# A 4096 x 4096 matmul with GELU: one partial product of the first group moved forward, set aside and put back into PSUM

## The chip, the cores and the metric

One core of a Trainium2 chip. The metric is the device time of one execution in microseconds (us), the median of several. Engine names: PE is the matmul engine (PEld its weight loads), DVE the vector engine, ACT the scalar engine, POOL the engine that issues most loads, SP the one that issues stores.

## The reference

```
x = np.matmul(a, b)               # a, b: 4096 x 4096, float32
return 0.5 * x * (1 + np.tanh(np.sqrt(2 / np.pi) * (x + 0.044715 * x**3)))
```

The result is 4096 x 4096 in float32.

## The kernel before

A and B are each cut into four quarters, A11 to A22 and B11 to B22, and most of the output is made with Strassen's seven products (M1 to M7) instead of eight. Operands are float16, sums in PSUM are float32. The output is made in groups: a group takes 512 rows of each half of A (four tiles of 128 rows, `i` from 0 to 3) and 512 columns of each half of B, and makes four blocks, c11, c12, c21 and c22. There are 4 by 4 groups; inside a group the 2048-long sum is cut into two chunks of 1024 (`c` = 0 and 1). So "A12_0" is A12's first chunk for the group, "A12_1" its second. The whole program is written in Python as a list of `steps`; for each step the lists `before` and `tasks` hold the loads, transposes and sums that are issued ahead of that step's matmuls. Each engine runs its instructions in the order in which they are written.

**The first group** differs from the others. While its data still come in, its first chunk is multiplied without Strassen: eight plain products (`PLAIN`), each of two steps, steps 0 to 15, in `plain` (matmuls on L524, 16 in a step). Its second chunk then goes through Strassen's products, steps 16 to 29: M3, M5, M7, M1, M4, M2, M6, two steps each (`multiply`, matmuls on L493). Group 1 begins at step 30.

The plain products, in the kernel's order (`PLAIN`, L101): c12 by A11 B12; c11 by A11 B11; c21 by A21 B11; c12 by A12 B22; c11 by A12 B21; c21 by A22 B21; c22 by A21 B12; c22 by A22 B22. All products but those of c11 go through the same four PSUM banks ("Y", one for each row tile `i`); c11 has the other four ("X"). Between two products in Y the banks must be read out:

- c12's first part: copied by ACT into tiles x1 (`keep`, L604); its second part: added to them by DVE (`tt`, L646).
- c11: both parts are summed in the X banks, and DVE then adds them to x1's tiles.
- c21's first part: copied by ACT (L540); its second part: added by DVE.
- c22: both parts, being neighbours, are summed in PSUM, and DVE subtracts the sum from x1's tiles.

The products with `True` in their last place go by rows: their first step makes the row tiles 0 and 1 in full, the second the tiles 2 and 3. The others make half of the sum for all four tiles in each step.

**Loading.** A line of the table at L761, such as `(9, "T22_0 W22_0 A12_1+B21_1a B21_1b")`, names what is issued ahead of a step: `A..`/`B..` a load, `T..` a transpose, `W..` weighing, `S..` a sum of two blocks of B. All loads are issued by POOL in the order written (L280); a load that must wait for its buffer holds back those behind it.

- `load_a` brings a chunk of A (1 MB as float16) into a stage tile. There are two stage tiles (`bufs=2`), used in turn. The one exception is `THIRD = ("22", 1)`: A22_1 goes into the four tiles "x7", which hold M7's parts later; in the profile these are named x.
- `turn_a` (T) transposes it on DVE into the block that PE reads (L244).
- `weigh_first` (W) squares each of the 16 rows of blocks in the stage tile on ACT, in place, with a sum along the row (L294; an ACTIVATE and a read of the accumulator for each of 16). It is part of a check of the inputs' sizes, on which the kernel's path depends. Only when all 16 are done is the stage tile free for the next load.

So the chunk that takes a stage tile next waits for the squares of the chunk before: A22_0 for W21_0, A11_1 for W12_0, A12_1 for W22_0, A21_1 for W11_1.

`make_sums` (L455) makes Strassen's sums of blocks on DVE; by default the loop at the end of `half_path` calls it two steps ahead (`AHEAD = 2`). The first of them, for M3, is B12_1 + B22_1; M5 needs A11_1 - A12_1, M7 needs A12_1 - A22_1 and B21_1 + B22_1, and M1 (A11_1 - A22_1 and B11_1 - B22_1) is the first to need B11_1.

Of the kernel before, what the change touches and what calls it, by code (L numbers as in the profile page):

```python
# [22 lines left out]
RT = 4  # L23
# [76 lines left out]

PLAIN = [  # L101
    ("12", "11", "12", False), ("11", "11", "11", False), ("21", "21", "11", True),
    ("12", "12", "22", False), ("11", "12", "21", False), ("21", "22", "21", True),
    ("22", "21", "12", True), ("22", "22", "22", True),
]
N_PLAIN = 2 * len(PLAIN)

# [1 line left out]
C21_FIRST = (0, 5, QPH - 1)  # L109
# [50 lines left out]
def half_path(  # L160
# [9 lines left out]
    nc = tc.nc  # L170
# [243 lines left out]
    kept = {}  # L414
# [57 lines left out]
    N_RAW = NNB + 2  # L472
# [3 lines left out]
    post = {}  # L476
# [21 lines left out]
    def warm():  # L498
        z = pool.tile([P, NC], F16, name="zeros", tag="bS", bufs=AHEAD + 1)
        nc.vector.memset(z[:, :], 0.0)  # L500
        for i in range(RT):
            bank(0, "X", i)
            bank(0, "Y", i)
        for _ in range(N_WARM):
            nc.tensor.matmul(
                banks["X", RT - 1][:, :], z[:, :P], z[:, :], start=True, stop=True, skip_group_check=True
            )

    def plain(n):

        (quad, oa, ob, by_rows), h = PLAIN[n // 2], n % 2
        chain = "X" if quad == "11" else "Y"
        seen = [x for x in range(len(PLAIN)) if PLAIN[x][0] == quad]
        sa, sb = a_tiles[0, oa, 0], b_tiles[0, ob, 0]
        sa = sa.rearrange("p jj (m e) -> p jj m e", e=2)
        tiles = [(j, e) for j in range(NJ // 2) for e in range(2) if by_rows or e == h]
        for i in range(h * RT // 2, (h + 1) * RT // 2) if by_rows else range(RT):
            acc = banks[chain, i]
            kept = quad in ("11", "22")
            start = (n // 2 == seen[0] or not kept) and (by_rows or h == 0)  # L520
            stop = (n // 2 == seen[-1] or not kept) and (by_rows or h == 1)
            c = f"c{quad}"
            for j, e in tiles:
                nc.tensor.matmul(  # L524
                    acc[:, :], sa[:, j, i * P : (i + 1) * P, e], sb[:, 2 * j + e, :],
                    start=start and (j, e) == tiles[0], stop=stop and (j, e) == tiles[-1],
                    skip_group_check=True,
                )
            if not stop:
                continue  # L530
            if not kept and n // 2 == seen[1]:
                tt(post[c, i], post[c, i], acc, ALU.add)
            elif quad == "12":
                post[c, i] = keep("x1", acc, RT)
            elif quad == "11":
                tt(post["c12", i], post["c12", i], acc, ALU.add)
            elif quad == "21":
                tag = ("energy1", "energy2", "square", "square")[i]
                t = pool.tile([P, W], BF16, name="c21", tag=tag, bufs=1 + (i > 1)).bitcast(F32)
                nc.scalar.copy(out=t[:, :], in_=acc[:, :])  # L540
                post[c, i] = t
            else:
                tt(post["c12", i], post["c12", i], acc, ALU.subtract)

# [57 lines left out]
    def keep(tag, src, bufs):  # L602
        t = pool.tile([P, NC], F32, name=tag, tag=tag, bufs=bufs)
        nc.scalar.copy(out=t[:, :], in_=src[:, :])  # L604
        return t
# [39 lines left out]
    def tt(o, x, y, op):  # L645
        nc.vector.tensor_tensor(out=o[:, :], in0=x[:, :], in1=y[:, :], op=op)  # L646
# [84 lines left out]
    for gi in range(1, len(groups)):  # L731
        s = 0
# [9 lines left out]
    before = {}  # L742

    def step_number(gi, s, q):
        gi, s = gi + s // NP, s % NP
        if (gi, s, q) in position:
            return position[gi, s, q]
        s0 = max(x for x in SPLITS if x <= s)
        return position[gi, s0, PAIR[0][1]] + (s - s0) * len(SPLIT) + 2 * q
# [10 lines left out]

    for n, whats in (  # L761
        (0, "A11_0 B12_0 T11_0 W11_0 B11_0 A21_0 A12_0 B22_0 B21_0"),
        (4, "T21_0 W21_0 A22_0"),
        (6, "T12_0 W12_0"),
        (8, "A11_1+B12_1+B22_1"),
        (9, "T22_0 W22_0 A12_1+B21_1a B21_1b"),
        (14, "T11_1 W11_1 A22_1 B11_1"),
        (16, "T12_1"),
        (17, "A21_1"),
        (18, "S2 S3 T22_1 W22_1:0-4"),  # L770
        (19, "W22_1:4-8"),
        (20, "W22_1:8-12"),
        (21, "W22_1:12-16"),
        (23, "T21_1"),
        (34, "W12_1:0-1"),
        (35, "W12_1:1-2"),
        (36, "W12_1:2-3"),
        (37, "W12_1:3-4"),
        (38, "W12_1:4-5"),
        (39, "W12_1:5-6"),  # L780
        (40, "W12_1:6-7"),
        (41, "W12_1:7-8"),
        (42, "W12_1:8-9"),
        (43, "W12_1:9-10"),
        (44, "W12_1:10-11"),
        (45, "W12_1:11-12"),
        (46, "W12_1:12-13"),
        (47, "W12_1:13-14"),
        (48, "W12_1:14-15"),
        (49, "W12_1:15-16"),  # L790
        (50, "W21_1:0-1"),
        (51, "W21_1:1-2"),
        (52, "W21_1:2-3"),
        (53, "W21_1:3-4"),
        (54, "W21_1:4-5"),
        (55, "W21_1:5-6"),
        (56, "W21_1:6-7"),
        (57, "W21_1:7-8"),
        (58, "W21_1:8-9"),
        (59, "W21_1:9-10"),  # L800
        (60, "W21_1:10-11"),
        (61, "W21_1:11-12"),
        (62, "W21_1:12-13"),
        (63, "W21_1:13-14"),
        (64, "W21_1:14-15"),
        (65, "W21_1:15-16"),
    ):
        for what in whats.split():
            half = what[-1] == "0" and what != "A11_0" or what in ("A22_1", "T22_1")
            if what[0] == "S":  # L810
                before.setdefault(n, []).append((make_sums, (0, 2, int(what[1]), "bS")))
                continue
            if what[0] == "W":
                xs = range(*(int(x) for x in what[6:].split("-"))) if what[6:] else range(NX)
                before.setdefault(n, []).append((weigh_first, (what[1:3], int(what[4]), xs)))
                continue
            for h in (0, 1) if half else (None,):
                args = [
                    (x[0], (0, x[1:3], int(x[4]), "ab".index(x[5]) if x[5:] else h))
                    for x in what.split("+")  # L820
                ]
                if what[0] == "T":
                    before.setdefault(n, []).append((turn_a, args[0][1]))
                    if what == "T22_1":
                        for q in range(QPH // 2, QPH):
                            before[n].append((make_sums, (0, 2, q, "aS", h)))
                else:
                    pairs = [({"A": load_a, "B": load_b}[x], xs) for x, xs in args]
                    before.setdefault(n, []).append((load, pairs))
# [57 lines left out]
    for nb, gi in last_raw.items():  # L887
# [6 lines left out]
        for x, piece in enumerate(pieces):  # L894
            n = position[gi, 0, 0] + max(x // 2, x - n_two)
            if two:
                n = position[gi - 1, 0, 0] + TWO_GROUPS[x]
# [251 lines left out]
    for gi in range(N_RAW, len(groups)):  # L1149
# [5 lines left out]
        for made, first_s, first_q, made_nb, name in MAKES:  # L1155
            s0, x = PLACE[name]
            ps = [p for p in SPLIT if not isinstance(SPLIT[p][2], str)]
            n = step_number(made, first_s, first_q)
# [4 lines left out]
        for n in mine:  # L1163
            _, s, q = steps[n]
# [33 lines left out]
    with tc.manual_schedule():  # L1198
        warm()
        table = pool.tile([P, 1], F32, name="table", tag="table")  # L1200
        nc.vector.memset(table[:, :], 0.0)
        nc.scalar.activation(table[:, :], table[:, :], ACT.Gelu_apprx_tanh)
        for n, step in enumerate(steps):
            for fn, args in before.get(n, ()):
                fn(*args)
            if n + AHEAD < len(steps):
                gi, s, q = steps[n + AHEAD]
                if s >= 0 and gi < N_RAW and step != C21_FIRST:
                    make_sums(gi, s, q)
            for fn, args in tasks.get(n, ()):  # L1210
                fn(*args)
            if step[:2] != (0, 2):
                flush()
            combine()
            if step[1] < 0:
                plain(n)
            elif step[2] in SPLIT:
                multiply_split(*step)
            else:
                multiply(*step)  # L1220
            if step == C21_FIRST:
                make_sums(*steps[n + AHEAD])
            if step == (0, 2, QPH - 1):
                flush()
        flush()
# [3 lines left out]
def kernel(tc: tile.TileContext, a: bass.AP, b: bass.AP, out: bass.AP):  # L1229
    stands = half_path(tc, a, b, out)  # L1230
    with tc.If(stands == 0):
        general_path(tc, a, b, out)
# [30 lines left out]
```

## Time and profile before

| | |
|---|---|
| median of 8 runs | 1558.95 us (1554.63 to 1563.45) |
| the profiled execution, its own time | 1560.27 us |
| its span, first to last instruction | 1558.6 us |
| granted PE clock, mean | 0.999 |

| stretch (us) | PE busy | DVE busy | ACT busy | POOL busy | GB/s |
|---|---|---|---|---|---|
| 38 to 60 | 22.00 | 10.25 | 9.94 | 16.85 | 192 |
| 70 to 76 | 6.00 | 4.75 | 2.23 | 4.54 | 195 |
| 76 to 83 | 7.00 | 6.67 | 3.49 | 6.70 | 126 |
| 83 to 90 | 6.60 | 5.16 | 5.50 | 5.93 | 155 |

Rows of the profile in order of time read: start in us, duration in us, engine, line, operation, output<-input, shape, count, and in square brackets the idle time of that engine just before, with what ended it. Rows of waits read: the engine, what it was to write, its line, what it waited for, then us in total, times, and the longest. A line such as L646 is a helper's and is used from many places; the names of the tiles tell which. PE's ends are modelled, so two neighbouring rows may overlap by some tenths of a microsecond.

### The profile page before, as it was taken

Reading aid. Unit: us, or ns where it says so; the run is one execution under the profiler, and the core shown is the slowest. Engines: PE = TensorE matmul, PEld = TensorE weight load, DVE = VectorE, ACT = ScalarE, POOL = GpSimd, SP = SyncE. Lnnn points to the kernel's source line nnn. Section 1 sums busy time; section 2 is a strip of 40 time slices with the busy share of each in tenths; the row PEclk is TensorE's granted clock in tenths of the full one; section 3 lists DMA queues with packets and bytes.
Section 4 is the critical chain, followed back from the end, with each engine's and each line's share of the span. In section 5 each row is a group of like instructions: output and inputs, shape, how many; then the busy total and the mean of one; then the engine's idle time right before and its main releaser. Section 6 shows DMA issues by size and latency. Waiting matters only on the chain. (4 is left out here: it accounts for less than half of the span.)

```text
span 1558.6 us, 22302 instructions
## 1 busy us (share of the span) xinstructions
PE 1543.9 (99%) x8110; PEld 793.7 (51%) x8110; DVE 1139.8 (73%) x1359; ACT 600.7 (39%) x1323; POOL 464.0 (30%) x830
## 2 busy tenths in 40 slices
PE   9999999999999999999999999999998999999998
PEld 4444444444444444444444444645646457677674
DVE  1598888999878888755657667867739677867674
ACT  5347555366633641211543211122344423232232
POOL 7764333431123211222322211211333212132130
PEclk9999999999999999999999999999999999999999
DMA  9999999994799988999799988868999958688693
GB/s 177 191 206 263 299 316 289 291 211 82 207 252 290 303 290 306 360 375 326 199 341 279 415 305 340 313 267 272 303 202 342 325 181 286 235 281 314 232 331 115
DMA packets 201909, 425.21 MB, mean 273 GB/s; under 512 B 20416, under 2 KB 102592, under 8 KB 199744
## 3 DMA queue, kind: packets, MB, share of 16 engines
q0 software_dynamic: 140448, 261.15, 65.7%
q1 hardware_dynamic: 61200, 162.43, 27.4%
q8 instruction: 66, 1.08, 0.3%
q14 instruction: 51, 0.42, 0.1%
q10 hardware_dynamic: 144, 0.13, 0.0%
HBM read 336.60 MB, written 162.53 MB: 320 GB/s over the span
## 5 line engine op out<-in xcount | busy, mean ns | idle before, releaser
L493 PEld LDWEIGHTS <-aS 128*128 128x128 f16 x4192 | 409.6, 98 | 497.3 <-issue 3.4
L493 PE MATMUL accX<-bK,aS 128*128 128x512 f16 x1536 | 334.0, 379 | 0.0
L976 DVE TENSOR_TENSOR aS<-aT 128x2048 f16<-128x2048 f16 x182 | 217.6, 1221 | 94.6 <-PE accX L493 63.0
L493 PEld LDWEIGHTS <-aT 128*128 128x128 f16 x1600 | 156.6, 98 | 188.1
L962 POOL DMA_DIRECT2D bK<-k_M x228 | 121.0, 535 | 419.4 <-PE accX L493 116.9
L280 POOL DMA_DIRECT2D bR<-in_b_dram x320 | 173.7, 546 | 215.0 <-DMA bR<-in_b_dram 96.5
L294 ACT ACTIVATE stage<-stage 128x512 f16<-128x512 f16 (+1 forms) x304 | 163.3, 542 | 112.6 <-DVE aT L244 78.7
L493 PE MATMUL accY<-bK,aS 128*128 128x512 f16 x896 | 195.2, 379 | 0.4 <-DVE x L646 0.3
L637 ACT ACTIVATE x<-x 128x512 f32<-128x512 f32 x124 | 75.7, 629 | 236.6 <-DVE x L646 236.6
L455 DVE TENSOR_TENSOR aS<-aT 128x2048 f16<-128x2048 f16 (+1 forms) x112 | 134.2, 1202 | 29.8 <-PE accX L493 18.6
L575 PEld LDWEIGHTS <-aS 128*128 128x128 f16 x1440 | 141.4, 98 | 27.4 <-issue 4.5
L493 PE MATMUL accX<-bS,aS 128*128 128x512 f16 x704 | 153.3, 379 | 0.4 <-ACT m L604 0.4
L455 DVE TENSOR_TENSOR bS<-bR 128x2048 f16<-128x2048 f16 x110 | 133.7, 1220 | 21.4 <-PE accX L493 13.6
L604 ACT COPY x<-accX 128x512 f32<-128x512 f32 x116 | 67.5, 586 | 194.5 <-PE accX L493 193.8
L336 ACT ACTIVATE square<-bR 128x1024 bf16<-128x1024 f16 x120 | 123.1, 1050 | 42.1 <-DVE energy L646 40.9
L244 DVE STREAM_TRANSPOSE aT<-stage 128x1024 uint32<-128x1024 uint32 (+1 forms) x59 | 73.5, 1279 | 70.8 <-DMA stage<-in_a_dram 70.8
L280 POOL DMA_DIRECT2D stage<-in_a_dram x136 | 80.2, 595 | 138.4 <-ACT stage L294 100.7
L976 DVE TENSOR_TENSOR bS<-bK 128x2048 f16<-128x2048 f16 x70 | 84.4, 1219 | 25.6 <-DMA k_split<-bS 25.5
L493 PE MATMUL accY<-bK,aT 128*128 128x512 f16 x448 | 97.8, 379 | 0.0
L493 PE MATMUL accX<-bK,aT 128*128 128x512 f16 x448 | 97.8, 379 | 0.0
L604 ACT COPY m<-accX 128x512 f32<-128x512 f32 x76 | 43.5, 582 | 126.2 <-PE accX L493 100.3
L646 DVE TENSOR_TENSOR x<-accY,x 128x512 f32<-128x512 f32 x116 | 77.5, 689 | 17.9 <-ACT y L637 11.1
(76 smaller groups left out, 1539.1 us busy)
## 6 DMA issues: line engine op xcount, KB each, us to landing
bK<-k_M POOLq DMA_DIRECT2D x264, 512.0 KB, 9.7
bK<-k_split POOLq DMA_DIRECT2D x90, 512.0 KB, 6.5
bR<-in_b_dram POOLq DMA_DIRECT2D x320, 128.0 KB, 7.6
k_M<-bS SPq DMA_DIRECT2D x80, 512.0 KB, 6.7
k_split<-bS SPq DMA_DIRECT2D x70, 512.0 KB, 7.0
out_dram<-y SPq DMA_DIRECT2D x131, 256.0 KB, 6.1
out_dram<-x SPq DMA_DIRECT2D x124, 256.0 KB, 7.1
stage<-in_a_dram POOLq DMA_DIRECT2D x112, 256.0 KB, 9.0
```

Of the source, the lines that this page charges most:

```text
L244: nc.vector.transpose(dst[:, :, x, :], src)
L280: nc.gpsimd.dma_start(out=dst, in_=src)
L294: nc.scalar.activation(src, src, ACT.Square, accum_out=dst)
L336: nc.scalar.activation(t[:, :], src, ACT.Square)
L455: nc.vector.tensor_tensor(out=x, in0=y, in1=z, op=ALU.add if o[2] > 0 else ALU.subtract)
L493: nc.tensor.matmul(acc[:, :], sa[:, j // 2, i * P : (i + 1) * P, j % 2], sb[:, j, :], start=start and j == 0, stop=stop and j == 3, skip_g ...
L575: nc.tensor.matmul(banks[chain, i][:, :] if wide else out, sa[:, j // 2, r * P : (r + 1) * P, j % 2], sb[:, : NC] if wide else sb[:, j * N ...
L604: nc.scalar.copy(out=t[:, :], in_=src[:, :])
L637: nc.scalar.activation(y[:, :], src[:, :], ACT.Gelu_apprx_tanh)
L646: nc.vector.tensor_tensor(out=o[:, :], in0=x[:, :], in1=y[:, :], op=op)
L962: nc.gpsimd.dma_start(out=dst, in_=kept_unit(*key[1:])[:, x * w : (x + 1) * w])
L976: nc.vector.tensor_tensor(out=t, in0=y, in1=z, op=ALU.add if op > 0 else ALU.subtract)
```

## The change

Four things, all in the first group:

1. A21 by B12 (c22's first part) moves from the seventh to the fourth place among the plain products. c12's second, c11's second and c21's second part each move one place back. A22 by B22 stays last.
2. c22's two parts are no longer neighbours in the Y banks. The first is copied by ACT into tiles of the tag x7 after steps 6 and 7; just ahead of A22 by B22 (steps 14 and 15) ACT copies it back into the Y banks, and the matmuls add to it.
3. The table of what is issued ahead of which step is rewritten: the squares of A21_0 are spread over steps 4 to 7, T12_0 and W12_0 stand at step 8 instead of 6, T22_0 at 12 instead of 9, the squares of A22_0 are spread over steps 13 to 16, A12_1's load stands ahead of B21_1's instead of being interleaved with its first half, A22_1's and B11_1's loads are at 12 instead of 14, and T11_1 at 15 instead of 14.
4. M3's sums are no longer made two steps ahead by the loop but by new entries: S02 at step 15, S03 at 16 (the sums of B alone), X02 and X03 at 16 (the rest of `make_sums`, which finds the sum made).

A22_1's stage in the x7 tiles is in the kernel before already; `THIRD` isn't touched.

```
 PLAIN = [
     ("12", "11", "12", False), ("11", "11", "11", False), ("21", "21", "11", True),
-    ("12", "12", "22", False), ("11", "12", "21", False), ("21", "22", "21", True),
-    ("22", "21", "12", True), ("22", "22", "22", True),
+    ("22", "21", "12", True), ("12", "12", "22", False), ("11", "12", "21", False),
+    ("21", "22", "21", True), ("22", "22", "22", True),
 ]
...
-            stop = (n // 2 == seen[-1] or not kept) and (by_rows or h == 1)
+            stop = (n // 2 == seen[-1] or quad != "11") and (by_rows or h == 1)
             c = f"c{quad}"
+            if quad == "22" and not start:
+                nc.scalar.copy(out=acc[:, :], in_=post.pop((c, i))[:, :])
...
                 post[c, i] = t
+            elif start:
+                post[c, i] = keep("x7", acc, RT)
             else:
                 tt(post["c12", i], post["c12", i], acc, ALU.subtract)
...
         (0, "A11_0 B12_0 T11_0 W11_0 B11_0 A21_0 A12_0 B22_0 B21_0"),
-        (4, "T21_0 W21_0 A22_0"),
-        (6, "T12_0 W12_0"),
-        (8, "A11_1+B12_1+B22_1"),
-        (9, "T22_0 W22_0 A12_1+B21_1a B21_1b"),
-        (14, "T11_1 W11_1 A22_1 B11_1"),
-        (16, "T12_1"),
+        (4, "T21_0 W21_0:0-2 A22_0"),
+        (5, "W21_0:2-6"),
+        (6, "W21_0:6-11"),
+        (7, "W21_0:11-16"),
+        (8, "T12_0 W12_0 A11_1+B12_1+B22_1"),
+        (9, "A12_1 B21_1"),
+        (12, "T22_0 A22_1 B11_1"),
+        (13, "W22_0:0-6"),
+        (14, "W22_0:6-8"),
+        (15, "T11_1 S02 W22_0:8-10"),
+        (16, "S03 X02 X03 W22_0:10-16 W11_1 T12_1"),
         (17, "A21_1"),
-        (18, "S2 S3 T22_1 W22_1:0-4"),
+        (18, "S22 S23 T22_1 W22_1:0-4"),
...
             if what[0] == "S":
-                before.setdefault(n, []).append((make_sums, (0, 2, int(what[1]), "bS")))
+                before.setdefault(n, []).append((make_sums, (0, int(what[1]), int(what[2]), "bS")))
+                continue
+            if what[0] == "X":
+                before.setdefault(n, []).append((make_sums, (0, int(what[1]), int(what[2]))))
                 continue
...
-                if s >= 0 and gi < N_RAW and step != C21_FIRST:
+                if s >= 0 and gi < N_RAW and step != C21_FIRST and (gi, s) != (0, 0):
                     make_sums(gi, s, q)
```

## The prediction

> **What bounds the kernel now.** I read the page first, then PE's waits up to 220 us, then PE, DVE, POOL and ACT in order of time up to 125 us. PE is the bound:
>
> ```profile
> span 1558.6 us, 22302 instructions
> PE 1543.9 (99%) x8110; PEld 793.7 (51%) x8110; DVE 1139.8 (73%) x1359; ACT 600.7 (39%) x1323; POOL 464.0 (30%) x830
> ```
>
> The matmuls stay as they are, so only PE's idle time (1558.6 - 1543.9 = 14.7 us) can move. PE's waits up to 220 us, apart from the one for the first instruction (us, times, longest):
>
> ```profile
> PE accY L524 <- DMA bR<-in_b_dram: 1.3, 2, 0.8
> PE accY L493 <- DVE x L646: 1.1, 1, 1.1
> PE accY L493 <- DVE bS L455: 0.5, 1, 0.5
> PE accX L493 <- ACT m L604: 0.4, 1, 0.4
> ```
>
> They add up to 3.3 us, the most that can be gained. From 120 to 220 us PE has no gap, so a shift of PE at 120 us stays to the end. PE in order of time:
>
> ```profile
> 27.34 7.07 PE L524 MATMUL accY<-bR,aT 128*128 128x512 f16 x32
> 35.24 7.07 PE L524 MATMUL accY<-bR,aT 128*128 128x512 f16 x32 [0.83 <-DMA bR<-in_b_dram]
> 49.05 20.88 PE L524 MATMUL accY<-bR,aT 128*128 128x512 f16 x96
> 69.77 7.07 PE L493 MATMUL accY<-bS,aT 128*128 128x512 f16 x32
> ```
>
> A product of 32 matmuls takes 6.9 us, a step 3.45. The 0.83 us is a wait for B22_0. DVE:
>
> ```profile
> 49.76 2.44 DVE L646 TENSOR_TENSOR x<-x,accX 128x512 f32<-128x512 f32 x4
> 63.32 2.31 DVE L244 STREAM_TRANSPOSE aT<-stage 128x2048 uint32<-128x2048 uint32 x1 [6.41 <-DMA stage<-in_a_dram]
> 71.88 2.31 DVE L244 STREAM_TRANSPOSE aT<-stage 128x2048 uint32<-128x2048 uint32 x1 [1.22 <-DMA stage<-in_a_dram]
> 89.99 1.22 DVE L455 TENSOR_TENSOR bS<-bR 128x2048 f16<-128x2048 f16 x1 [1.70 <-DMA bR<-in_b_dram]
> ```
>
> DVE waits for the loads A11_1, A12_1 and B11_1. From 90 to 120 us it is busy 29.9 of 30 us, and PE's gaps at 112 and 117 us are waits for it: loads set DVE, DVE sets PE. POOL issues the loads:
>
> ```profile
> 1.56 2.73 POOL L280 DMA_DIRECT2D stage<-in_a_dram  x4 [0.88 <-POOLq L1247]
> 11.08 2.45 POOL L280 DMA_DIRECT2D bR<-in_b_dram  x4 [0.83 <-DMA stage<-in_a_dram]
> ...
> 59.62 0.66 POOL L280 DMA_DIRECT2D stage<-in_a_dram  x1 [0.31 <-issue]
> ...
> 64.05 0.66 POOL L280 DMA_DIRECT2D stage<-in_a_dram  x1
> ...
> 66.05 1.18 POOL L280 DMA_DIRECT2D bR<-in_b_dram  x2 [0.78 <-DMA stage<-in_a_dram]
> ...
> 72.03 7.54 POOL L280 DMA_DIRECT2D x<-in_a_dram  x13 [0.82 <-DMA stage<-in_a_dram]
> ...
> 80.41 4.30 POOL L280 DMA_DIRECT2D bR<-in_b_dram  x8
> ```
>
> 59.62 and 64.05 are A12_1's first and fourth piece, 66.05 is eight issues after the first, 72.03 eight after the fourth; each ends a wait for that piece's landing (72.03 beside DVE's 71.88). So about eight loads are out at once, and they move 192 to 200 GB/s from 14 to 70 us with DMA busy throughout: 1 MB takes 5.4 us.
>
> **The change, part by part.** PE's steps 0 to 7 start as now (step n at 13.53 + 3.45 n).
>
> *A21 by B12 fourth.* A12 by B22 starts at 41.2 instead of 35.2 us, after B22_0 has landed: -0.83.
>
> *Setting aside.* Four ACT copies at 0.58 (as c21's at L540, mean 583 ns) in steps 6 and 7. ACT's order becomes W21_0's squares (16 by 0.40) in parts between the copies: bank 3 is read by 41.8, and PE writes it again at 43.8. Hidden with 2.0 us to spare. W21_0 ends at 40.3 instead of 32.1, so A22_0's issue slips from 38.9 to 40.3; W12_0, now behind the copies, ends at 48.2 instead of 41.4, so A11_1's first issue slips from 45.55 to 48.2. About eight outstanding loads (5 us of work) cover both; uncovered they would cost 1.4 and 2.7.
>
> *T22_0 moved to step 12.* Step 12 is A22 by B21 and needs it at once. DVE works in program order (49.76: the adds are behind T22_0 today), so the transpose now follows the four adds of step 11, and the last add needs the last matmul of step 11. Add 0.27 us after PE (from the adds at 41.55 and 42.42), 0.62 each in a row, 1.25 a transposed half, 0.05 back: **+2.2 us** of PE idle, step 12 at 57.2. Bounds: 0, excluded by the order, and 3.4 if both halves counted. Net now +1.4.
>
> *Putting back.* Four ACT copies into PSUM. No row has this size; 128x256 into PSUM takes 376 ns (L597) and out of it 367 to 373 (L592), so 0.59 each. Step 13's PE ends at 64.1; c21's adds end at 59.8, 61.6, 63.3 and 65.1, the copies at 61.0, 62.2, 63.9 and 65.7, while PE needs bank 0 at 64.1 and bank 3 at 69.3: hidden by 3 us and more. The page "PSUM — Partial Sum Buffer" of the Trainium skill (Summary: rules for kernel authors) speaks against the part: a seed written by ScalarE must be 0, because such writes don't set the accumulation flags; here step 12's matmuls have written the same elements, and no run here shows the flags. Adding after eviction instead would be four DVE adds, 2.5 us by their rows.
>
> *T11_1 behind the subtractions of step 14, then S02.* The second subtraction follows PE's step 14 (67.55): 67.8 to 68.5, transpose 2.31, sum 1.2: M3 starts at 72.05 where PE is ready at 71.0: **+1.0**. PE stands at +2.3.
>
> *W22_0 in parts over steps 13 to 16: the price.* The two stage buffers alternate, so A12_1 needs the one that W22_0 reads. Today W22_0 ends at 53.5 and POOL reaches A12_1 at 59.6. Now its last six squares stand behind the last put-back: 65.7 + 2.4 = **68.1 us**. POOL waits there some 8 us, and B21_1, A22_1, B11_1, A21_1 stand behind it. The outstanding loads run out near 65, data flow again about 1.7 us after the issue (in the start: issue 1.56, first bytes 3.3). A12_1 has all landed at 68.1 + 1.7 + 5.4 + 0.5 = 75.7, or, as A11_0 in the start (1.56 to 10.9), at 77.5; today 71.9. Then with eight outstanding loads: B21_1's eight land every 0.67 us until 81.1 or 82.9, each letting a piece of A22_1 go, whose last eight cost POOL 0.57 each: B11_1 is issued from 86.2 or 88.0 instead of 80.4: **+5.8 to +7.6 us**. DVE's wait at 89.99 for B11_1 moves by as much (it has 1.7 us of slack there, and its own chain from A12_1 is late by less), and from there to 120 us it has no idle time to give back. PE's stalls of 2.2 and 1.0 lie within this, they don't add.
>
> Outer bounds for B11_1: POOL's issues alone after 68.1 (4 by 0.66, 8 by 0.55, 16 by 0.57, 8 by 0.54 = 20.5 us) end at 88.6 against 84.7: +3.9. The same 30.4 us as today from A12_1's first issue to DVE's sum: 98.5, +8.5. I take **+6.5**, between the two chains. S02, S03, X02, X03 and S22, S23 are the same sums as now in other places: no cost beyond the above. "A third place" for A22_1 is already there (THIRD, the x tiles at 70 to 80 us); it now shares its four tiles with the set-aside parts, free at 65.7, long before its turn.
>
> Sum on the profiled execution: 1560.27 + 6.5 = 1566.8 us (span 1565.1). It is 1.3 above the median of the eight runs, so on the median: 1558.95 + 6.5 = **1565.5 us**.
>
> **Rivals.** Measurement tells about 0.2%, 3.1 us, from no change.
>
> *Not slower: the loads catch up.* After POOL's wait the DMA engines are empty. If they then move the late 4 MB faster than 195 GB/s, and POOL's small pieces of A22_1 don't hold B11_1 up, DVE's wait at B11_1 vanishes. What stays is A12_1's lateness: PE's 2.3 us at M3 less the 1.7 of slack, +0.8 to +2.5: 1560 to 1561.5. It decides if B11_1 lands by 92.5. For it: from 160 to 170 us the core moves 370 GB/s. Against it: no slice from 14 to 76 us is above 234 GB/s with this kind of load, and 76 to 83 is at 126, POOL's own pace. The Trainium skill's "DMA: Bandwidth & Descriptors" (Anatomy of one DMA) gives about 2.0 us plus bytes at 436 GB/s; by that 1 MB is an estimated 2.4 us, not 5.4, and this rival would come true; the rows above decide against it.
>
> *Faster.* A12_1 and T22_0 wait for nothing that I see, and only the removed stalls count: -0.8 to -3.3, 1555.7 to 1558.1. It needs the engines to run out of program order, which no row shows.
>
> *Slower still.* The restart takes today's 30.4 us and DVE's lateness opens new gaps of PE in the second group's first sums: +8.5 to +12, 1567.5 to 1571.
>
> *It doesn't do what it says.* The third place is old; if the set-aside hid nothing, only -0.83 is lost, inside every case.
>
> **How the numbers follow.** Forecast (+3.5 to +8.5) 0.72; slower still 0.06; loads catch up 0.17; the faster rival 0.05, of which only the end beyond -3.1 counts as faster, 0.02. Slower by over 0.2%: 0.72 + 0.06 = 0.78; within it 0.17 + 0.03 = 0.20; faster 0.02. The range runs from 1560 (takes in most of the catching up) to 1570.
>
> **What would show it.** Right: no gap before step 8; a PE gap of 2.2 us near 55 us ended by T22_0; M3 1.0 us behind its operands; POOL idle some 8 us until 68, ended by ACT's last square of W22_0; a hole in DMA near 65 to 70; T12_1 at 75.7 to 77.5; DVE's sum on B11_1 at 95.8 to 97.6; PE's total idle up by 6.5. Wrong: A12_1 issued near 60, T22_0 ahead of step 11's adds, or B11_1's sum by 92.5.

## The result and the profile after

The changed kernel is slower: 1566.65 us, median of 19 runs (1561.22 to 1572.5), against 1557.25 us of 56 runs of the kernel before; ratio of the means 1.0056, 95% interval 1.0044 to 1.0068, or +8.7 us (6.9 to 10.6). The medians alone differ by 9.4. The prediction was 1565.5 us, +6.5, and 0.78 for slower: the direction and the time came true, the amount lies just below the interval. The profiled execution took 1568.57 us.

The first two rows of the page, then PE's waits up to 220 us:

```profile
span 1566.9 us, 22315 instructions
PE 1546.8 (99%) x8110; PEld 794.2 (51%) x8110; DVE 1140.6 (73%) x1359; ACT 605.5 (39%) x1331; POOL 463.8 (30%) x830
```

```profile
PE accX L493 <- DVE aS L455: 4.4, 2, 2.7
PE accY L526 <- DVE aT L244: 1.9, 1, 1.9
...
PE accY L493 <- DVE bS L455: 1.1, 2, 0.7
PE accX L493 <- ACT m L608: 0.4, 1, 0.4
PE accY L493 <- DVE x L650: 0.3, 1, 0.3
```

PE still does 8110 matmuls; ACT has eight instructions more, the four copies out and the four back. The wait for a load of B is gone from PE's list. In its place stand waits for DVE's transposes (aT) and sums (aS, bS). PE in order of time shows where, with the same start of group 1 in the kernel before below it:

```profile
27.46 20.88 PE L526 MATMUL accY<-bR,aT 128*128 128x512 f16 x96
48.18 7.07 PE L526 MATMUL accX<-bR,aT 128*128 128x512 f16 x32
57.19 13.99 PE L526 MATMUL accY<-bR,aT 128*128 128x512 f16 x64 [1.94 <-DVE aT L244]
71.83 7.07 PE L493 MATMUL accY<-bS,aT 128*128 128x512 f16 x32 [0.65 <-DVE bS L455]
81.59 8.55 PE L493 MATMUL accX<-bR,aS 128*128 128x512 f16 x32 [2.69 <-DVE aS L455]
...
128.18 13.98 PE L493 MATMUL accY<-bS,aT 128*128 128x512 f16 x64
```

```profile
120.76 13.98 PE L493 MATMUL accY<-bS,aT 128*128 128x512 f16 x64
```

96 matmuls from 27.46 without a gap: the 0.83 us for B22_0 has gone. Then come 1.94 us before step 12, 0.65 before M3, 2.69 before M5 (the 1.70 within M7 isn't shown). The start of group 1 has moved from 120.76 to 128.18 us: **7.4 us** of the change stand there, and PE has only one other gap above 0.4 us after it, the 3.8 us that it had before. This start is the mark for all that follows. A whole execution is a poor mark: the 19 of this kernel spread over 11 us.

ACT's last square of A22_0 and POOL's loads of A12_1, A22_1 and B11_1:

```profile
67.69 0.41 ACT L294 ACTIVATE stage<-stage 128x256 f16<-128x256 f16 x1
67.99 0.19 ACT L294 ACTIVATION_READ_ACCUMULATOR stage<-stage 128x1 f32 x1
```

```profile
40.90 4.68 POOL L280 DMA_DIRECT2D stage<-in_a_dram  x8 [3.00 <-ACT stage L294]
...
48.75 0.66 POOL L280 DMA_DIRECT2D stage<-in_a_dram  x1 [2.08 <-ACT stage L294]
...
68.48 2.56 POOL L280 DMA_DIRECT2D stage<-in_a_dram  x4 [7.41 <-DVE x L650]
...
82.65 5.45 POOL L280 DMA_DIRECT2D x<-in_a_dram  x10 [0.16 <-issue]
88.08 4.30 POOL L280 DMA_DIRECT2D bR<-in_b_dram  x8
```

A12_1 goes out at 68.48 instead of 59.62, B11_1 at 88.08 instead of 80.41. The bracket at 68.48 names a DVE add that ended at 68.45, by accident: the read behind the last square ended at 68.18, and POOL went on 0.3 us later, as it did after the squares that released it at 40.90 (end 40.61) and 48.75 (end 48.46). The first experiment settles it. DVE at its two waits for loads:

```profile
77.96 2.31 DVE L244 STREAM_TRANSPOSE aT<-stage 128x2048 uint32<-128x2048 uint32 x1 [3.85 <-DMA stage<-in_a_dram]
...
97.41 1.23 DVE L455 TENSOR_TENSOR bS<-bR 128x2048 f16<-128x2048 f16 x1 [0.69 <-issue]
```

T12_1 is 6.1 us later than before, the sum on B11_1 7.4 us, just what PE has lost at group 1. Ahead of that sum the profile names nothing that DVE waited for (`issue`); that it was the load is read from the time: the sum starts 9.3 us after B11_1's first issue, and 9.6 before the change, where the load is named. The stretches (us; PE, PEld, DVE, ACT, POOL busy with counts; granted clock, DMA share, GB/s):

```profile
38.00:60.00 22.00, 20.06 (x93) 8.90 (x92) 8.47 (x11) 12.82 (x59) 14.78 (x27) 1.00 1.20 169
60.00:65.00 5.00, 5.00 (x25) 2.28 (x24) 2.00 (x3) 3.04 (x11) 1.07 (x2) 1.00 1.32 201
65.00:70.00 5.00, 5.00 (x25) 2.29 (x24) 2.99 (x4) 3.03 (x13) 1.52 (x3) 1.00 0.18 30
70.00:76.00 6.00, 5.35 (x26) 2.35 (x25) 4.11 (x5) 5.24 (x27) 4.28 (x8) 1.00 1.29 166
76.00:83.00 7.00, 4.31 (x18) 1.74 (x17) 4.67 (x3) 1.26 (x7) 4.71 (x9) 0.87 1.24 192
```

Two things are seen: the hole from 65 to 70 us, 30 GB/s instead of 197, which was predicted, and a weaker one from 38 to 60, 169 instead of 192, which was not. The clock of 0.87 is taken up at the end.

### The profile page after: what moved, and what is told of

The parts are those of the page before. It is cut to its first block, busy times and chain, and to the rows that moved or that the text cites. A ratio compares the mean times of both kernels' runs of the same rounds, so it can differ in the third digit from the quotient of the medians.

```text
span 1566.9 us, 22315 instructions
## 1 busy us (share of the span) xinstructions
PE 1546.8 (99%) x8110; PEld 794.2 (51%) x8110; DVE 1140.6 (73%) x1359; ACT 605.5 (39%) x1331; POOL 463.8 (30%) x830
## 3 DMA queue, kind: packets, MB, share of 16 engines
q8 instruction: 66, 1.08, 0.3%
## 5 line engine op out<-in xcount | busy, mean ns | idle before, releaser
L641 ACT ACTIVATE x<-x 128x512 f32<-128x512 f32 x124 | 75.7, 629 | 237.4 <-DVE x L650 237.4
L650 DVE TENSOR_TENSOR x<-accY,x 128x512 f32<-128x512 f32 x116 | 77.5, 689 | 17.8 <-ACT y L641 11.1
```

What stands on the lines that cost most here:

```text
L641: nc.scalar.activation(y[:, :], src[:, :], ACT.Gelu_apprx_tanh)
```

## The experiments

Theory 1 is the prediction's: A22_0's last squares hold A12_1 on POOL, all loads behind it are late, DVE follows B11_1 and PE follows DVE. Theory 2: PE's own gaps (T22_0, T11_1) are the price, and the late load hides. The results, each timed in five rounds; times of the marks in us, from the profiles:

| kernel | ratio to before (95%) | A12_1's first issue | B11_1's first issue | group 1 on PE | difference of the last two |
|---|---|---|---|---|---|
| before | 1 | 59.62 | 80.41 | 120.76 | 40.35 |
| changed | 1.0056 (1.0044 to 1.0068) | 68.48 | 88.08 | 128.18 | 40.10 |
| 1: squares early | 1.0029 (1.0014 to 1.0045) | 63.84 | 83.80 | 123.86 | 40.06 |
| 2: transpose early | 1.0026 (1.0014 to 1.0039) | 66.09 | 85.44 | 125.52 | 40.08 |
| 3: transpose early, squares late | 1.0054 (1.0033 to 1.0076) | 69.62 | 88.85 | 129.12 | 40.27 |
| 4: B21 first | 1.0022 (1.0008 to 1.0037) | 68.03 | 82.46 | 124.08 | 41.62 |
| 5: no put-back | 1.0028 (1.0008 to 1.0047) | 63.59 | 83.23 | 123.81 | 40.58 |
| 6: transpose and squares early | 1.0011 (0.9994 to 1.0028) | 62.43 | 82.91 | 123.23 | 40.32 |
| 7: placed as before | 1.0017 (0.9998 to 1.0037) | 62.28 | 82.67 | 123.16 | 40.49 |
| 8: before, with a late load | 1.0061 (1.0042 to 1.0079) | 68.57 | 89.00 | 129.34 | 40.34 |
| 9: early squares too | 1.0013 (0.9996 to 1.0029) | 59.54 | 80.13 | 120.54 | 40.41 |
| 10: early squares alone | 1.0062 (1.0040 to 1.0085) | 68.50 | 88.33 | 128.88 | 40.55 |

The last column is the finding: in eleven of these twelve kernels group 1 starts 40.1 to 40.6 us after B11_1's first issue, whatever gaps PE had before. DVE is the link between the two: from the start of its sum on B11_1 (89.99 before, 97.41 in the changed kernel) to the start of group 1 it is 30.74 to 30.77 us in all twelve. Each mark comes from one profiled execution, and the first product doesn't start at the same time in all; counted from that start, the differences from the changed kernel shift by at most 0.5 us, in 3 by 1.3. Edits of 1 to 7 and 10 are against the changed kernel, that of 9 against 7.

**1, squares early.**

```
-        (13, "W22_0:0-6"),
-        (14, "W22_0:6-8"),
-        (15, "T11_1 S02 W22_0:8-10"),
-        (16, "S03 X02 X03 W22_0:10-16 W11_1 T12_1"),
+        (13, "W22_0"),
+        (15, "T11_1 S02"),
+        (16, "S03 X02 X03 W11_1 T12_1"),
```

> The changed kernel, but all 16 squares of A22_0 stand at step 13, ahead of the put-backs; T22_0 stays at step 12. Mark used in all runs: the start of group 1 on PE, 120.8 us in the kernel before, 128.2 in the changed one. Theory 1 (A12_1's load is held on POOL by the last squares, and with it the loads behind it; DVE, then PE, follow B11_1): the squares end near 63.8, A12_1 is issued at 63.9 instead of 68.5, group 1 starts at 123 to 124.5, the whole 4 us shorter than the changed kernel. Theory 2 (PE's own gaps for T22_0 and T11_1 are the price, the late load is hidden): no change, 128.2, or 0.3 later for put-backs that come late.

PE's gap of 1.94 us before step 12 stays, and 4.3 us are gained at group 1. POOL in order of time:

```profile
63.84 2.55 POOL L280 DMA_DIRECT2D stage<-in_a_dram  x4 [2.40 <-ACT stage L294]
...
83.80 4.29 POOL L280 DMA_DIRECT2D bR<-in_b_dram  x8
```

The load follows the squares to 63.84, though the add named in the changed kernel's bracket still starts at 67.72. Theory 2 falls for the larger part of the time.

**2, transpose early, and 3, the same with more squares behind the last put-back.** 2 moves T22_0 to step 11; 3 also gathers squares 5 to 15 at step 16.

```
-        (12, "T22_0 A22_1 B11_1"),
+        (11, "T22_0"),
+        (12, "A22_1 B11_1"),
```

> The changed kernel, but T22_0 stands at step 11, ahead of that step's four adds; the squares of A22_0 stay where they are. Both theories: PE's gap of 1.9 us before step 12 is gone. Theory 1: the put-backs and the last squares come 1.9 us earlier with PE, A12_1 at 66.5, group 1 at 126.3. Theory 2: 126.3 too. This run prices the move; the next one tells the theories apart.

> As the run before (T22_0 at step 11, PE's gap before step 12 gone), but 11 of A22_0's 16 squares instead of 6 stand behind the last put-back, so that A12_1 is issued at about 68.5 as in the changed kernel. Theory 1: nothing gained, group 1 at 128 plus or minus 0.4, PE waits 1.9 us longer ahead of M5. Theory 2: 126.3, as in the run before.

In 2 the gap went and group 1 gained 2.7 us, A12_1 2.4. In 3 the same gap went and nothing was gained. PE of 3:

```profile
56.36 13.98 PE L526 MATMUL accY<-bR,aT 128*128 128x512 f16 x64
70.99 7.07 PE L493 MATMUL accY<-bS,aT 128*128 128x512 f16 x32 [0.65 <-DVE bS L455]
82.31 8.56 PE L493 MATMUL accX<-bR,aS 128*128 128x512 f16 x32 [4.26 <-DVE aS L455]
```

No gap before step 12, and 4.26 us before M5 instead of 2.69. This run began with a first product 1.27 us later (14.92 against 13.65), which is why A12_1 and group 1 are about 1 us later than expected. Counted from that start, A12_1's issue is at 54.7 against 54.8 in the changed kernel, and group 1 at 114.2 against 114.5. So the transpose costs what it does by delaying the put-backs and with them the squares, not by PE's gap.

**4, B21 first.**

```
-        (9, "A12_1 B21_1"),
+        (9, "B21_1 A12_1"),
```

> The changed kernel, but B21_1's load is written ahead of A12_1's. Theory 1 (POOL's whole queue is held): B21_1 goes out from 61 to 66, DMA has no hole, A12_1 is issued at 68.5 as before, A22_1 and B11_1 some 4 us earlier; group 1 at 123.5 to 125.5. A variant of it, that A12_1's own lateness sets DVE and the loads behind it don't matter: 127.5 to 128.2. Theory 2: 128.2.

A12_1 is as late as in the changed kernel, yet 4.1 us are gained (3.7 counted from the first product): about half of the change's time is what stood idle behind it. The stretch that had 30 GB/s, here:

```profile
65.00:70.00 5.00, 5.00 (x25) 2.29 (x24) 3.37 (x3) 2.74 (x13) 3.60 (x7) 1.00 1.24 202
```

It is also the one kernel off the 40.3 us: B11_1 is out at 82.46, but group 1 follows 41.6 later. PE and DVE show why:

```profile
81.13 7.08 PE L493 MATMUL accX<-bR,aS 128*128 128x512 f16 x32 [2.67 <-DVE aS L455]
```

```profile
77.50 2.31 DVE L244 STREAM_TRANSPOSE aT<-stage 128x2048 uint32<-128x2048 uint32 x1 [3.84 <-DMA stage<-in_a_dram]
...
93.33 1.22 DVE L455 TENSOR_TENSOR bS<-bR 128x2048 f16<-128x2048 f16 x1
```

DVE waits 3.84 us for A12_1. From then on it has no idle time, and its sum on B11_1 (93.33) starts when its own work is done, not when the load has landed. So here A12_1 sets the pace through DVE. Its own lateness is thus worth 3.3 us (124.08 - 120.76; 3.6 counted from the first product) when the loads behind it aren't held.

**5, no put-back.** This kernel changes what is computed: PSUM's Y banks go on from step 15 into M3, so without the put-back A21's and B12's first part is missing in the blocks made there.

```
-            start = (n // 2 == seen[0] or not kept) and (by_rows or h == 0)
+            start = (n // 2 == seen[0] or quad != "11") and (by_rows or h == 0)
...
-            if quad == "22" and not start:
-                nc.scalar.copy(out=acc[:, :], in_=post.pop((c, i))[:, :])
+            if quad == "22" and n // 2 == seen[1]:
+                tt(post["c12", i], post["c12", i], post.pop((c, i)), ALU.subtract)
...
-            elif start:
+            elif n // 2 == seen[0]:
```

> The changed kernel without the put-back: A22 by B22 starts afresh in PSUM, and DVE subtracts the set-aside part with four more adds (2.5 us) before step 14, where it has gaps. The squares of A22_0 stand where they are, but nothing on ACT waits for PE any more. Theory 1: the squares end near 63.8, A12_1 at 64, group 1 at 123 to 124.5. Theory 2: 128.2 or later, since DVE has more to do.

The squares stand where the change put them, but with no put-back among them to wait for PE, A12_1 goes out at 63.59 and group 1 starts at 123.81, as in 1. It is the put-back's wait for PE, passed on in ACT's order, that makes the squares late.

**6 and 7.** 6 moves T22_0 and all squares to step 10. 7 also puts T11_1 and S02 at 14, S03 at 15, and writes A12_1's load as before (`A12_1+B21_1a B21_1b`). The edit of 6:

```
-        (12, "T22_0 A22_1 B11_1"),
-        (13, "W22_0:0-6"),
-        (14, "W22_0:6-8"),
-        (15, "T11_1 S02 W22_0:8-10"),
-        (16, "S03 X02 X03 W22_0:10-16 W11_1 T12_1"),
+        (12, "A22_1 B11_1"),
+        (10, "T22_0 W22_0"),
+        (15, "T11_1 S02"),
+        (16, "S03 X02 X03 W11_1 T12_1"),
```

> The changed kernel with T22_0 and all squares of A22_0 at step 10; order of the products, set-aside, put-back and the place of T11_1 stay. Theory 1: POOL reaches A12_1 near 61 and doesn't wait, DMA has no hole; group 1 at 120.3 to 121.8, the time that of the kernel before within 1 us. Theory 2: only PE's gap of 1.9 us goes, 126.3.

> The new order of products with set-aside and put-back, but T22_0 and the squares at step 10, T11_1 and S02 at 14, S03 at 15, and A12_1's load interleaved with B21_1's first half as in the kernel before. If the loads set the pace, the 0.83 us that PE no longer waits for B22_0 come back as a wait for DVE at M6: group 1 at 120.0 to 120.8, no difference from the kernel before that can be measured. If PE's gaps set it: 119.2 and 1 to 1.5 us faster than before.

Both missed: group 1 at 123.2, above both expected ranges and 2.4 us later than in the kernel before, though nothing waits for A22_0's squares any more (the last ends before 58 us). POOL issued A12_1 only at 62.4 and 62.3. Of POOL in 7:

```profile
40.81 4.67 POOL L280 DMA_DIRECT2D stage<-in_a_dram  x8 [1.59 <-ACT stage L294]
...
48.66 0.65 POOL L280 DMA_DIRECT2D stage<-in_a_dram  x1 [2.09 <-ACT stage L294]
```

It had been held at A22_0 (1.59 us) and A11_1 (2.09) by the squares of A21_0 and A12_0, the waits that the prediction had costed at nothing. DMA moved 179 GB/s from 38 to 60 us in 7.

**8, the kernel before with a late load.** Only one square is moved:

```
-        (9, "T22_0 W22_0 A12_1+B21_1a B21_1b"),
-        (14, "T11_1 W11_1 A22_1 B11_1"),
+        (9, "T22_0 W22_0:0-15 A12_1+B21_1a B21_1b"),
+        (14, "T11_1 W11_1:0-6 W22_0:15-16 W11_1:6-16 A22_1 B11_1"),
```

> The kernel before, order of products and all, except that A22_0's last square stands behind six of A11_1's squares, so that A12_1's load is issued near 68.7 instead of 59.6. Theory 1: this alone makes most of the change's time, group 1 at 126.5 to 128.5, 6 to 8 us slower than before. Theory 2: the late load is hidden, group 1 at 121 to 122.

POOL and PE of this kernel:

```profile
68.57 0.66 POOL L280 DMA_DIRECT2D stage<-in_a_dram  x1 [9.87 <-ACT stage L294]
```

```profile
69.52 7.07 PE L493 MATMUL accY<-bS,aT 128*128 128x512 f16 x32
83.79 9.16 PE L493 MATMUL accX<-bR,aS 128*128 128x512 f16 x32 [7.20 <-DVE aS L455]
```

M3 starts as before the change, without any of its gaps; one square of 0.4 us on ACT behind the wrong neighbours costs 8.6 us at group 1 and as much as the whole change. The late load is enough.

**9 and 10, the early squares.** Into kernel 7 (9) and into the changed kernel (10), the same edit:

```
-        (4, "T21_0 W21_0:0-2 A22_0"),
-        (5, "W21_0:2-6"),
-        (6, "W21_0:6-11"),
-        (7, "W21_0:11-16"),
-        (8, "T12_0 W12_0 A11_1+B12_1+B22_1"),
+        (4, "T21_0 W21_0 A22_0"),
+        (6, "T12_0 W12_0:0-3"),
+        (7, "W12_0:3-7"),
+        (8, "W12_0:7-16 A11_1+B12_1+B22_1"),
```

> The seventh kernel (new order of products, set-aside, put-back, the rest placed as before) left 2.4 us at the start of group 1 (123.2 against 120.8), though A12_1 no longer waits for squares. Its A22_0 and A11_1 loads still wait for the squares of A21_0 and A12_0 behind the set-aside copies, and DMA moves 179 GB/s from 38 to 60 us against 192. Here W21_0 stands whole at step 4 and W12_0 between the copies from step 6 on. Theory 1a (those two waits cost DMA the 2.4 us, against the prediction's 0): A11_1's first piece is issued near 45.7, A12_1 near 59.6, DMA at 190 GB/s or more from 38 to 60, group 1 at 120 to 121. Theory 1b (something else in the new order costs it, such as DVE's order around T11_1): 122.5 to 123.5.

> The changed kernel with only that early part mended (W21_0 whole at step 4, W12_0 between the copies); T22_0, A22_0's squares and all else as changed, so A12_1 is still issued near 68.4. If POOL's long wait at A12_1 swallows what the early waits cost (the larger of the two counts): group 1 at 127.7 to 128.4, nothing gained. If the two add up: 125.5 to 126.

POOL of 9, and its stretch from 38 to 60 us:

```profile
45.84 0.65 POOL L280 DMA_DIRECT2D stage<-in_a_dram  x1 [0.81 <-ACT stage L294]
...
59.54 0.65 POOL L280 DMA_DIRECT2D stage<-in_a_dram  x1 [0.68 <-DVE c L650]
...
80.13 4.29 POOL L280 DMA_DIRECT2D bR<-in_b_dram  x8
```

```profile
38.00:60.00 22.00, 22.00 (x104) 9.98 (x103) 9.16 (x12) 14.35 (x63) 16.80 (x30) 1.00 1.33 199
```

These loads are back within 0.3 us of where they were before the change, and group 1 is at 120.54, 2.6 us earlier than in 7. The first product starts at the same time in both (13.55 and 13.57), so the early waits are what was missing in 7 (theory 1a); the ratios of whole executions, 1.0013 and 1.0017, are too coarse to show it. In 10 the same edit gains nothing (128.88, 0.5 above the range expected for that case): POOL gets to A12_1 sooner and waits longer there, 9.02 us instead of 7.41. The two holds don't add up; the later one swallows the earlier.

Kernel 9 has the change's new order, set-aside and put-back without its price, and keeps the 0.83 us: M3 starts at 68.80 instead of 69.77. At group 1 0.2 us are left, as much as DVE's sum on B11_1 is earlier (89.77 against 89.99). PE gives most of the rest back in a new wait for DVE at M7, and still waits at M6, where it waited 1.08 us before:

```profile
83.49 0.59 PE L493 MATMUL accX<-bS,aS 128*128 128x512 f16 x2 [0.72 <-DVE aT L244]
...
113.02 3.61 PE L493 MATMUL accY<-bS,aS 128*128 128x512 f16 x16 [0.82 <-DVE x L650]
```

Its ratio, 1.0013 (0.9996 to 1.0029), can't be told from no change. No version that I ran beats the kernel before.

## Why the prediction was right, and where a step failed

- **B22_0's wait, -0.83**: gone, as said. The sum rightly didn't count it: kernel 9 has it and starts group 1 only 0.2 us earlier.
- **Setting aside.** PE was not held, right. That the outstanding loads cover the slips of A22_0 and A11_1 was **wrong**: the slips were 2.0 and 3.2 us (40.90 and 48.75; forecast 40.3 and 48.2), DMA fell to 169 GB/s from 38 to 60 us (to between 116 and 167 from 40 to 48, where it was 167 to 202 before), and alone they cost 2.6 us at group 1 (7 against 9), near the 2.7 that the prediction gave for the larger slip uncovered. In the changed kernel the error did no harm, because the longer hold at A12_1 hides it (10).
- **T22_0 at step 12**: 1.94 us, forecast 2.2. Its mechanism, behind the adds of step 11, was right; experiment 3 shows that the gap itself costs nothing while the late load sets the pace.
- **Put-back**: 0.58 to 0.59 us each, hidden from PE, as forecast. The alternative that I priced, four adds after eviction, was misread: the Y banks' sums aren't finished at step 15, since M3 adds to them (experiment 5).
- **T11_1 behind the subtractions**: 0.65, forecast 1.0.
- **W22_0 and A12_1, the price**: issue at 68.48 (forecast 68.1), T12_1 at 77.96 (75.7 to 77.5), B11_1 from 88.08 (86.2 to 88.0), DVE's sum at 97.41 (95.8 to 97.6). Taken +6.5, measured 7.4. The path was right; the size was taken between a restart at full rate and one like the start's, and the restart was like the start's: 9.5 us from A12_1's first issue to its transpose, 9.4 for A11_0 in the start. The 0.3 us from the last read to the issue were left out too.
- **The rest**: the two profiled spans differ by 8.3 us, of which 7.4 stand at group 1 (0.1 of it is a later first product). PE's later waits for DVE account for 0.6 more; the 0.3 left are less than two executions of one kernel differ by. PE's idle time rose by 5.4 us and not by 6.5: the other 2.9 are busy time, which the prediction had taken as fixed, and 1.5 of them are M5 at a lower clock (last section).
- **The time**, 1566.65 against 1565.5, is closer than its parts: the kernel before came out at 1557.25 in the later runs instead of 1558.95, which offset most of the too small amount. That is luck.
- **The rival "loads catch up"** is refuted: from A12_1's issue to B11_1's it takes 19.6 us in the changed kernel and 20.8 before, 1.2 us caught up of 8.9. The Trainium skill's page "DMA: Bandwidth & Descriptors" (Anatomy of one DMA), 436 GB/s, spoke for that rival; no stretch shown above is over 202 GB/s. In that rival's own sum, 2.3 less 1.7 is 0.6, not 0.8; nothing rests on it.

## What to carry to other kernels

Where one engine issues all loads in order, look for the load that waits longest for its buffer and ask which engine frees it and what that engine does just before: here a check off the critical path, placed behind a copy that waits for the matmuls, held a load for 7.4 us and cost the kernel as much. Outstanding loads cover a hold only if the rate stays up, so read the DMA rate of the stretch and not only the matmul engine's gaps. When two holds follow each other in one queue, count the larger and not their sum (seen here once, in 10), and try a mark such as "the next group's start minus the last load's issue": if it is constant over many edits, look there first; the edit that breaks it (4) shows what comes next, here DVE's own work.

## What the runs showed of the hardware that I had not expected

After some long gaps PE came back with a lower granted clock. M5 in 10 (compare its row in 4, above):

```profile
81.79 8.48 PE L493 MATMUL accX<-bR,aS 128*128 128x512 f16 x32 [2.87 <-DVE aS L455]
```

M5's 32 matmuls took 8.55 us behind a gap of 2.69 us in the changed kernel, 8.48 behind 2.87 (10), 8.56 behind 4.26 (3) and 9.16 behind 7.20 (8), but 7.08 behind gaps of 2.67 (4) and 2.39 (2), with the clock at 1.00. In the changed kernel the granted clock was 0.50 from about 81.2 to 84.6 us: it fell some 2.3 us into the gap and came back 3.4 us later. In 10 it fell 2.3 us into the gap, in 3 3.9 and in 8 4.6. Gaps of 2.67 and 2.69 us came out differently, so the length of the gap alone doesn't decide; what else does stays open here. In the changed kernel these 1.5 us are hidden, since M7 waits for DVE all the same. The page "TensorE: Matmul & The Clock Gate" of the Trainium skill (Part 1: The HAM clock gate) gives about 3.4 us as the idle time after which the clock falls; here it fell within a gap of 2.69.
